# Right-hand tiles shifted by 32 bytes, and the last MLP chunk's down product without Strassen's scheme

## The chip, the cores and the metric

The kernel runs on one core of a Trainium2 chip. The time is the device time of one execution in microseconds; several executions were timed and the median is given. A profile of one execution goes with it.

## The reference, cut to what matters

One layer on 512 tokens of 1,024 features, in float32. The first half: RMSNorm, one input projection into five parts, a recurrent branch (causal convolution, gated linear recurrence, times a GeLU gate) and a spatial-gating branch, merged by two sigmoid gates and projected back. The second half is a squared-ReLU MLP of width 4,096, then a final RMSNorm:

```python
h2 = rmsnorm(x, norm_ffn_g)
f = jnp.square(jax.nn.relu(jnp.einsum('bsd,df->bsf', h2, w_up)))
x = x + jnp.einsum('bsf,fd->bsd', f, w_down)
out = rmsnorm(x, final_norm_g)
```

## The kernel before, in words

Every large product is done in three float32r matmuls: each operand is split into a high part (rounded to float32r) and a low part (the rest), and high x high, high x low and low x high are summed in PSUM (`mm3`, lines 239 to 242). Every matmul of these products is 128x128 by 128x512.

**Places in SBUF.** Tile pools are opened on the left side, growing up from low addresses, or on the right side (`side="right"`), growing down from the top. On the right lie only `xp` in the first half (24 tiles of 2,048 bytes per partition: `xg0` to `xg7` high and low, and `u`) and, after it is closed, `x2p` in its place (24 tiles: the residual `xres0` to `xres7` and `x20` to `x27` high and low). In the compiled program these begin at 180,192 and every 2,048 bytes from there; 180,192 leaves 32 when divided by 64. The pools on the left hold the weights (`wp`: `wraw`, `whi`, `wlo`), the first half's other tiles (`tp`, with `ya`, `yb`, `mg`) and the MLP's (`mp`); their tiles that a product reads leave 0, and these addresses are no part of the change.

**First half.** `v` and `u` (lines 307 to 321) have tokens on the partitions: `xg` is the stationary operand and the weights stream. The column tiles that follow in the order of `ORDER` (lines 32 to 35 and 554 to 566) have weights as the stationary operand: `x`, `g`, `gb` and `ga` stream `xg` (8 k-tiles, 24 matmuls per column tile), `bb` streams `yb` (24), `ba` streams `ya` (10 k-tiles, 30 matmuls), and `o` streams `mg` (24).

**Weights.** A list of items gives the order in which PE uses 512 KB weight tiles. `item()` (line 217) takes the next one, splits up to three items ahead and issues loads up to five ahead, on SP's queue. A split is one ACT pass for the high part (line 116) and one DVE subtraction for the low part (line 117). Items for which `by_dma` (line 189) holds, all `up` weights of the MLP and some of its last chunk's others, have ACT write the high part and its negative (lines 207, 208), and a DMA issued by POOL adds the raw tile to it (line 209).

**MLP.** The width is cut into four chunks of 1,024. In a chunk c, eight `up` steps (24 matmuls, streaming `x2`) make `f`; `up_out` (line 615) evacuates them with DVE and ACT. The down product of a chunk is done on 2x2 blocks (two token halves, two halves of the chunk's width, two halves of the output) in Strassen's scheme, Winograd's form: seven products (`PRODUCTS`: p1, p2, p5, p6, p3, p7, p4) of 24 matmuls each. Sums of activation blocks (`factor`, line 643) and of weight blocks (`sum_item`, line 176) are made by DVE in place ahead of them. Each product's activation block is split into `fh` and `fl`, which have two buffers each. After each product, DVE adds its two PSUM banks to the residual `xk` (line 701). The `up` steps of chunk c+1 stand between the products of chunk c (`mlp_steps`, line 60). The last chunk has no `up` steps between its products.

**End.** `last` (line 725) squares the residual with a row sum on ACT as parts of it are complete, and `finish` (line 713) makes, for each block of 128 tokens, the root of the mean square (DVE, ACT, DVE), then the two halves of the output on DVE, and writes each with a DMA.

The order of instructions on an engine is laid down at build time by a planner that simulates them; on the chip each engine's queue runs in that order.

Of the kernel before, what the change touches and what calls it, by code (L numbers as in the profile page):

```python
# [52 lines left out]
PRODUCTS = ("p1", "p2", "p5", "p6", "p3", "p7", "p4")  # L53
HK = KT // 2
HT = T // 2

AHEAD = 120


def mlp_steps():  # L60

    steps = [("up", 0, j) for j in range(FT)]
    for c in range(NCH):
        more = [("up", c + 1, j) for j in range(FT)] if c + 1 < NCH else []
        for q in PRODUCTS:
            steps.append(("dn", c, q))
            steps += more[:1]
            more = more[1:]
        steps += more
    return steps  # L70

# [2 lines left out]
def trunk(ctx: ExitStack, tc: tile.TileContext, xT, wall, wdn, lruw, wsT, par, ln, out):  # L74
    nc = tc.nc
# [59 lines left out]
    mp = [None]  # L135
# [11 lines left out]
    n_first = n_units - NCH * FT  # L147
    items = [("u", u) for u in range(n_first)]
    steps = mlp_steps()
    for s in steps:  # L150
        if s[0] == "up":
            items.append(("u", n_first + s[1] * FT + s[2]))
        else:
            items += [("d", s[1], s[2], h) for h in range(2)]
    raws, ready, summed = {}, {}, set()
    dn_raw = {}
# [31 lines left out]

    def by_dma(n):

        kind = items[n][0]
        return n >= n_first and (kind == "u" or (items[n][1] == NCH - 1 and items[n][2] in ("p2", "p6", "p3", "p4")))

    def split_item(n, pieces=1):
        if n >= len(items) or n in ready:
            return
        hi = wp.tile([P, UB * P], F32R, tag="whi", name=f"whi{n}", bufs=4)
        lo = wp.tile([P, UB * P], F32R, tag="wlo", name=f"wlo{n}", bufs=4)
        if items[n][0] == "u":
            src = raws.pop(n)  # L200
        else:
            _, c, q, h = items[n]
            sum_item(n)
            src = dn_raw[c, {"p1": "b11", "p2": "b21", "p5": "b12", "p6": "b12", "p3": "b22", "p7": "b11", "p4": "b21"}[q], h]
        if by_dma(n):

            nc.scalar.activation(hi, src, AF.Copy)  # L207
            nc.scalar.activation(lo, hi.bitcast(F32), AF.Copy, scale=-1.0)  # L208
            nc.gpsimd.dma_start(out=lo, in_=src, accum_op=ALU.add)  # L209
        else:  # L210
            w = UB * P // pieces
            for i in range(pieces):
                sl = slice(i * w, (i + 1) * w)
                split(src[:, sl], hi[:, sl], lo[:, sl])
        ready[n] = (hi, lo)

    def item():
        n = pos[0]
        pos[0] += 1
        ready.pop(n - 1, None)  # L220
        ahead = 3 if n < n_first - 1 else 4
        for i in range(ahead):
            split_item(n + i)
        for i in range(ahead, ahead + 2):
            sum_item(n + i)
        for i in range(ahead, 6):
            load_item(n + i)
        return ready[n]
# [128 lines left out]
    lw = []  # L357
# [282 lines left out]
        tick()  # L640


    def factor(c, q):
        a = a_[c]
        if q in ("p5", "p6"):
            a["s" + q[1]] = mp[0].tile([P, HK, HT], F32, tag="fs", name=f"s{c}{q}", bufs=2)
        for out_, in0, in1, op in {
            "p5": [("s5", "a21", "a22", ALU.add)],
            "p6": [("s6", "s5", "a11", ALU.subtract)],
            "p3": [("a12", "a12", "s6", ALU.subtract)],  # L650
            "p7": [("a11", "a11", "a21", ALU.subtract)],
        }.get(q, []):
            nc.vector.tensor_tensor(out=a[out_], in0=a[in0], in1=a[in1], op=op)
        src = a[{"p1": "a11", "p2": "a12", "p5": "s5", "p6": "s6", "p3": "a12", "p7": "a11", "p4": "a22"}[q]]
        hi, lo = (mp[0].tile([P, HK, HT], F32R, tag=f"f{x}", name=f"f{x}{c}{q}", bufs=2) for x in "hl")
        split(src, hi, lo)
        return hi, lo

    fac, bank = {}, {}

    def ahead_of(i):

        for s in steps[i + 1 :]:
            if s[0] == "dn":
                c, q = s[1:]
                if (c, q) not in fac and made[c] >= (HK if q == "p1" else FT):
                    fac[c, q] = factor(c, q)
                return

    def down(i, c, q, done):  # L670
        if (c, q) not in fac:
            fac[c, q] = factor(c, q)

        k = {"p1": "d", "p6": "d", "p7": "d", "p4": "d", "p2": "e", "p5": "e", "p3": "e"}[q]
        first = q in ("p1", "p2", "p5")
        if first:
            bank[k] = [(pd if k == "d" else pe).tile([P, T], F32, tag=k, name=f"{q}{c}_{j}") for j in range(2)]
        w = [item(), None]
        fh, fl = fac.pop((c, q))
# [12 lines left out]
        mm(1, 0)  # L692
        w[1] = item()
        mm(0, 1)
        mm(1, 1)
        ahead_of(i)
# [5 lines left out]
        done(q)  # L702


    gfin = [None]
    s3 = const.tile([P, NB, 2], F32, name="s3")
    r3 = const.tile([P, NB], F32, name="r3")

    def square(b, h):
        sq = mp[0].tile([P, T], F32, tag="fs", name=f"sqc{b}_{h}", bufs=2)  # L710
        nc.scalar.activation(sq, xk[b][h], AF.Square, accum_out=s3[:, b, h : h + 1])

    def finish(b):
        nc.vector.tensor_tensor(out=r3[:, b : b + 1], in0=s3[:, b, 0:1], in1=s3[:, b, 1:2], op=ALU.add)
        nc.scalar.activation(r3[:, b : b + 1], r3[:, b : b + 1], AF.Sqrt, bias=eps_t, scale=1.0 / D)
        nc.vector.reciprocal(r3[:, b : b + 1], r3[:, b : b + 1])
        for h in range(2):
            o = mp[0].tile([P, T], F32, tag="fa", name=f"o{b}_{h}", bufs=4)
            nc.vector.scalar_tensor_tensor(
                out=o, in0=xk[b][h], scalar=r3[:, b : b + 1], in1=gfin[0][:, h * T : (h + 1) * T],  # L720
                op0=ALU.mult, op1=ALU.mult,
            )
            (nc.sync, nc.scalar)[h].dma_start(out=out[b * P : (b + 1) * P, h * T : (h + 1) * T], in_=o)

    def last(q):

        for b, h in {"p2": [(0, 0), (1, 0)], "p3": [(0, 1), (1, 1)], "p7": [(2, 1), (3, 1)], "p4": [(2, 0), (3, 0)]}.get(q, []):
            square(b, h)
        for b in {"p3": (0, 1), "p4": (2, 3)}.get(q, ()):
            finish(b)  # L730

    t_stack.close()
    ps_stack.close()
# [7 lines left out]
    for i, step in enumerate(steps):  # L741
        if step[0] == "up":
            up(*step[1:])
            ahead_of(i)
        else:
            down(i, *step[1:], last if step[1] == NCH - 1 else lambda q: None)
    assert pos[0] == len(items) and block[0] == UB


# [73 lines left out]
```

## Time and profile before

| | us |
|---|---|
| median of 3 runs | 817.94 (817.55 to 818.36) |
| the profiled execution | 817.47 |
| its span | 815.5 |
| PE busy | 799.1 (98%) |
| DVE busy | 502.7 (62%) |
| ACT busy | 474.4 (58%) |

The span runs from the first to the last instruction of the profiled execution; the execution's own time is 1.97 us longer. Busy times count an engine's instructions; a matmul's recorded duration reaches into the next ones, so the step from one start to the next tells PE's rate, not the duration.

### The profile page before, as it was taken

Reading aid. Unit: us, or ns where it says so; the run is one execution under the profiler, and the core shown is the slowest. Engines: PE = TensorE matmul, PEld = TensorE weight load, DVE = VectorE, ACT = ScalarE, POOL = GpSimd, SP = SyncE. Lnnn points to the kernel's source line nnn. Section 1 sums busy time; section 2 is a strip of 40 time slices with the busy share of each in tenths; the row PEclk is TensorE's granted clock in tenths of the full one; section 3 lists DMA queues with packets and bytes.
Section 4 is the critical chain, followed back from the end, with each engine's and each line's share of the span. In section 5 each row is a group of like instructions: output and inputs, shape, how many; then the busy total and the mean of one; then the engine's idle time right before and its main releaser. Section 6 shows DMA issues by size and latency. Waiting matters only on the chain.

```text
span 815.5 us, 9147 instructions
## 1 busy us (share of the span) xinstructions
PE 799.1 (98%) x3472; PEld 648.4 (80%) x3472; DVE 502.7 (62%) x656; ACT 474.4 (58%) x573; POOL 72.5 (9%) x83
## 2 busy tenths in 40 slices
PE   9999999999999999999999999999999999999975
PEld 7788888888888888888888877888888888888854
DVE  6767764876566667745544232965487647754675
ACT  7455437768788887772334644645555545554563
POOL 5100000000000000000003300000000000000110
PEclk9999999999999999999999999999999999999989
DMA  7633331213322322232224894466545664564345
GB/s 254 200 104 110 96 117 52 103 66 104 114 80 84 110 103 104 79 116 86 96 101 148 208 307 155 102 170 182 165 103 152 184 181 101 131 204 107 62 93 155
DMA packets 31867, 105.77 MB, mean 130 GB/s; under 512 B 3792, under 2 KB 3792, under 8 KB 31824
## 3 DMA queue, kind: packets, MB, share of 16 engines
q1 hardware_dynamic: 22608, 77.66, 27.1%
q0 software_dynamic: 5760, 20.97, 13.5%
q10 hardware_dynamic: 3456, 6.56, 2.6%
q8 instruction: 27, 0.44, 0.2%
q14 instruction: 16, 0.13, 0.0%
HBM read 82.11 MB, written 2.10 MB: 103 GB/s over the span
## 4 chain that ended last, share of the span: by engine, by line
PE 91%; DMA 3%; DVE 2%; issue 2%; ACT 2%; SPq 0%; DVEq 0%; POOL 0%; POOLq 0%; ACTq 0%
PE p L686 16%; PE up L240 7%; PE up L241 7%; PE up L242 7%; PE v L315 6%; PE u L315 5%; PE g L241 2%; PE g L242 2%; PE x L240 2%; PE x L241 2%; PE x L242 2%; PE g L240 2%; PE ba L240 2%; PE ba L242 2%; PE ba L241 2%; PE ga L242 2%
## 5 line engine op out<-in xcount | busy, mean ns | idle before, releaser
L116 ACT ACTIVATE whi<-wraw 128x1024 fp32r<-128x1024 f32 (+1 forms) x79 | 82.2, 1044 | 83.4 <-issue 24.3
L117 DVE TENSOR_TENSOR wlo<-wraw,whi 128x1024 fp32r<-128x1024 f32 (+1 forms) x79 | 97.3, 1233 | 27.9 <-ACT whi L116 27.5
L624 DVE SCALAR_TENSOR_TENSOR f<-up,r_b 128x512 f32<-128x512 f32 x32 | 21.9, 688 | 66.1 <-PE up L242 65.8
L207 ACT ACTIVATE whi<-wraw 128x1024 fp32r<-128x1024 f32 x32 | 33.6, 1051 | 42.0 <-PE up L241 26.7
L209 POOL DMA_DIRECT2D wlo<-wraw x32 | 27.6, 862 | 259.4 <-ACT wlo L208 234.8
L515 DVE SCALAR_TENSOR_TENSOR w<-w,s 128x512 f32<-128x512 f32 x10 | 6.9, 692 | 59.7 <-ACT w L510 59.7
L208 ACT ACTIVATE wlo<-whi 128x1024 fp32r<-128x1024 f32 x40 | 42.0, 1053 | 0.7
L701 DVE TENSOR_TENSOR xk<-p,xk 128x512 f32<-128x512 f32 x56 | 36.9, 683 | 5.4 <-PE p L686 5.4
L116 ACT ACTIVATE whi<-raw1b 128x1024 fp32r<-128x1024 f32 x14 | 14.9, 1062 | 25.4 <-PE up L241 15.6
L116 ACT ACTIVATE whi<-raw2b 128x1024 fp32r<-128x1024 f32 x14 | 14.9, 1061 | 24.5 <-PE up L241 15.6
L116 ACT ACTIVATE whi<-raw0b 128x1024 fp32r<-128x1024 f32 x14 | 14.8, 1058 | 22.4 <-PE up L241 15.3
L511 POOL TENSOR_TENSOR ig<-ig,xr 128x512 f32<-128x512 f32 x10 | 12.9, 1291 | 161.8 <-ACT ig L505 148.0
L686 PE MATMUL p<-whi,fh3p 128*128 128x512 f32 x56 | 22.7, 417 | 4.7 <-ACT fh3p L116 4.7
L628 ACT ACTIVATE f<-f 128x512 f32<-128x512 f32 x32 | 20.0, 626 | 7.7 <-DVE f L624 7.7
L117 DVE TENSOR_TENSOR wlo<-raw1b,whi 128x1024 fp32r<-128x1024 f32 x14 | 17.1, 1224 | 10.0 <-ACT whi L116 9.8
L686 PE MATMUL p<-wlo,fh3p 128*128 128x512 f32 x56 | 22.8, 406 | 0.5 <-DMA wlo<-raw3b 0.5
L479 DVE SCALAR_TENSOR_TENSOR xr<-xrp,par_sb,xr 128x512 f32<-128x512 f32 x30 | 22.5, 749 | 0.7
L117 DVE TENSOR_TENSOR wlo<-raw2b,whi 128x1024 fp32r<-128x1024 f32 x14 | 17.1, 1223 | 9.3 <-ACT whi L116 9.0
L485 ACT ACTIVATE xra<-xr 64x512 fp32r<-64x512 f32 x10 | 6.3, 632 | 27.3 <-DVE xr L479 27.3
L686 PE MATMUL p<-whi,fl3p 128*128 128x512 f32 x56 | 22.1, 407 | 0.0
L686 PE MATMUL p<-whi,fh0p 128*128 128x512 f32 x56 | 21.9, 391 | 0.0
L686 PE MATMUL p<-wlo,fh2p 128*128 128x512 f32 x56 | 21.8, 390 | 0.0
(852 smaller groups left out, 2445.5 us busy)
## 6 DMA issues: line engine op xcount, KB each, us to landing
wraw<-in_wall SPq DMA_DIRECT2D x109, 512.0 KB, 3.3
wlo<-wraw POOLq DMA_DIRECT2D x32, 512.0 KB, 4.5
raw0b<-in_wdn SPq DMA_DIRECT2D x8, 512.0 KB, 14.4
raw1b<-in_wdn SPq DMA_DIRECT2D x8, 512.0 KB, 4.1
raw2b<-in_wdn SPq DMA_DIRECT2D x8, 512.0 KB, 4.2
raw3b<-in_wdn SPq DMA_DIRECT2D x8, 512.0 KB, 4.3
wlo<-raw3b POOLq DMA_DIRECT2D x8, 512.0 KB, 4.6
xt<-in_xT SPq DMA_DIRECT2D x8, 256.0 KB, 6.5
```

Of the source, the lines that this page charges most:

```text
L116: nc.scalar.activation(hi, src, AF.Copy)
L117: nc.vector.tensor_tensor(out=lo, in0=src, in1=hi.bitcast(F32), op=ALU.subtract)
L207: nc.scalar.activation(hi, src, AF.Copy)
L208: nc.scalar.activation(lo, hi.bitcast(F32), AF.Copy, scale=-1.0)
L209: nc.gpsimd.dma_start(out=lo, in_=src, accum_op=ALU.add)
L240: nc.tensor.matmul(acc, lhs[0], rhs[0], start=start, stop=False)
L241: nc.tensor.matmul(acc, lhs[0], rhs[1], start=False, stop=False)
L242: nc.tensor.matmul(acc, lhs[1], rhs[0], start=False, stop=stop)
L315: nc.tensor.matmul(acc[b], xg[k][xi][:, b * P : (b + 1) * P], w[wi], start=k == 0 and i == 0, stop=k == KT - 1 and i == 2,)
L479: nc.vector.scalar_tensor_tensor(out=xr, in0=xrp[:, 1 + k : 1 + k + T], scalar=pc(C_CW + k * RT + j), in1=xr, op0=ALU.mult, op1=ALU.add)
L686: nc.tensor.matmul(bank[k][j], lhs[li], rhs[ri], start=first and kk == 0 and n == 0, stop=kk == HK - 1 and n == 2, skip_group_check=True,)
L701: nc.vector.tensor_tensor(out=x, in0=bank[k][j], in1=x, op=ALU.add)
```

## The change

A pool of one tile of 32 bytes per partition is opened on the right side ahead of all others there, so that every right-hand tile starts 32 bytes lower, at a multiple of 64.

In the MLP's last chunk the seven products are replaced by eight block products (`whole`), each over all four blocks of 128 tokens: for each half of the output (nh) and of the chunk's width (kh), two weight tiles (half) of 24 matmuls. No sums of blocks are made there. The activation blocks are split once each, four splits (`factor_whole`): the high parts take the buffers of `fh` (kh = 0) and `fl` (kh = 1), the low parts two buffers of `fa`. The accumulators are four banks, from `pe` for the first output half, and from `pd` and `pu` for the second. In the last of the four weight tiles of an output half the blocks of tokens end one by one, and each is added to the residual, squared and, in the second half, finished as it ends. The last chunk's `up` steps all stand ahead of chunk 2's p4, two of them after p3.

`by_dma` now holds only for the `up` weights of chunks 1 to 3; the first chunk's and all the last chunk's down weights are split by ACT and DVE. The splits and sums of activations are called from `item()`, by the item that is two (splits) or five (sums) ahead, and no longer after each step. In `finish` the first output half is made by ACT from the residual that DVE has multiplied by the final gain earlier, the second by DVE as before.

```diff
+        if c + 1 == NCH:
+            steps += [("whole", c, kh, nh, half) for nh in range(2) for kh in range(2) for half in range(2)]
+            break
...
+            if c + 2 == NCH and q == "p4":
+                steps += more
+                more = []
             steps.append(("dn", c, q))
-            steps += more[:1]
-            more = more[1:]
+            n = 2 if c + 2 == NCH and q == "p3" else 1
+            steps += more[:n]
+            more = more[n:]
...
+    padp = ctx.enter_context(tc.tile_pool(name="padp", bufs=1, side="right"))
+    pad = padp.tile([P, 8], F32, name="pad")
+    nc.vector.memset(pad, 0.0)
...
     def by_dma(n):
-        kind = items[n][0]
-        return n >= n_first and (kind == "u" or (items[n][1] == NCH - 1 and items[n][2] in ("p2", "p6", "p3", "p4")))
+        return n >= n_first + FT and items[n][0] == "u"
...
         ahead = 3 if n < n_first - 1 else 4
-        for i in range(ahead):
-            split_item(n + i)
-        for i in range(ahead, ahead + 2):
-            sum_item(n + i)
+        for i in range(6):
+            ahead_of(n + i, i < 3)
+            if i < ahead:
+                split_item(n + i)
+            else:
+                sum_item(n + i)
...
+    def factor_whole(c, kh):
+        if (kh, 0) in whole_f or made[c] < (kh + 1) * HK:
+            return
+        los = mp[0].tile([P, 2, HK, HT], F32R, tag="fa", name=f"lw{kh}", bufs=4)
+        for th in range(2):
+            src = a_[c][f"a{th + 1}{kh + 1}"]
+            hi = mp[0].tile([P, HK, HT], F32R, tag="fhfl"[2 * kh : 2 * kh + 2], name=f"fw{kh}{th}", bufs=2)
+            lo = los[:, th]
+            split(src, hi, lo)
+            whole_f[kh, th] = (hi, lo)
+
+    def hidden(n, whole):
+        if whole and n < len(items) and items[n][0] == "w":
+            factor_whole(items[n][1], int(items[n][2][1]) - 1)
+        if n < len(items) and items[n][0] == "d" and items[n][3] == 0:
+            c, q = items[n][1:3]
+            if made[c] >= (HK if q == "p1" else FT):
+                (factor if whole else factor_sum)(c, q)
...
+    def whole(c, kh, nh, half):
+        w = item()
+        if kh == 0 and half == 0:
+            for b in range(NB):
+                pool, tag = ((pe, "e"), (pd, "d"), (pu, "up"))[nh * (1 + b // 2)]
+                bank[b] = pool.tile([P, T], F32, tag=tag, name=f"w{nh}_{b}")
+        end = kh == 1 and half == 1
+
+        def mm(b, k):
+            fh, fl = (x[:, 2 * half + k, b % 2 * P : (b % 2 + 1) * P] for x in whole_f[kh, b // 2])
+            wh, wl = (x[:, k * T : (k + 1) * T] for x in w)
+            for n, (l, r) in enumerate(((fh, wh), (fh, wl), (fl, wh))):
+                nc.tensor.matmul(
+                    bank[b], l, r, start=kh == 0 and half == 0 and k == 0 and n == 0, stop=end and k == 1 and n == 2
+                )
+
+        if not end:
+            for k in range(2):
+                for b in range(NB):
+                    mm(b, k)
+            return
+        for b in range(NB):
+            for k in range(2):
+                mm(b, k)
+            x = xk[b][nh]
+            with tc.high_priority(offset=AHEAD):
+                nc.vector.tensor_tensor(out=x, in0=bank[b], in1=x, op=ALU.add)
+                square(b, nh)
+                if nh == 1:
+                    finish(b)
...
         for h in range(2):
-            o = mp[0].tile([P, T], F32, tag="fa", name=f"o{b}_{h}", bufs=4)
-            nc.vector.scalar_tensor_tensor(
-                out=o, in0=xk[b][h], scalar=r3[:, b : b + 1], in1=gfin[0][:, h * T : (h + 1) * T],
-                op0=ALU.mult, op1=ALU.mult,
-            )
+            o = og[b // 2][:, b % 2, h]
+            if h == 0:
+                nc.scalar.activation(o, xk[b][h], AF.Copy, scale=r3[:, b : b + 1])
+            else:
+                nc.vector.scalar_tensor_tensor(
+                    out=o, in0=xk[b][h], scalar=r3[:, b : b + 1], in1=gfin[0][:, T:], op0=ALU.mult, op1=ALU.mult
+                )
             (nc.sync, nc.scalar)[h].dma_start(out=out[b * P : (b + 1) * P, h * T : (h + 1) * T], in_=o)
```

## Rows read from the trace of the kernel before

**Rows 1.** The page, busy us (share of the span) xinstructions, and the chain that ended last.

```profile
PE 799.1 (98%) x3472; PEld 648.4 (80%) x3472; DVE 502.7 (62%) x656; ACT 474.4 (58%) x573; POOL 72.5 (9%) x83
...
PE 91%; DMA 3%; DVE 2%; issue 2%; ACT 2%; SPq 0%; DVEq 0%; POOL 0%; POOLq 0%; ACTq 0%
```

**Rows 2.** Waits of PE, whole span: who waited for whom, us, times, longest.

```profile
PE p L686 <- ACT fh3p L116: 4.7, 2, 3.5
PE up L240 <- DVE f L624: 1.9, 1, 1.9
...
PE p L686 <- DMA wlo<-raw3b: 0.5, 1, 0.5
```

**Rows 3.** Timeline of PE in u, gb and up: start us, us, instruction.

```profile
52.72 0.62 PE L315 MATMUL u<-whi,xg0h 128*128 128x512 f32 x2
...
97.52 0.39 PE L240 MATMUL gb<-xg0h,whi 128*128 128x512 f32 x1
...
187.65 0.39 PE L240 MATMUL gb<-xg0h,whi 128*128 128x512 f32 x1
...
193.27 0.39 PE L240 MATMUL g<-xg0h,whi 128*128 128x512 f32 x1
...
505.69 0.39 PE L240 MATMUL up<-x21h,whi 128*128 128x512 f32 x1
...
510.38 0.39 PE L242 MATMUL up<-x27h,wlo 128*128 128x512 f32 x1
```

**Rows 4.** Instructions on tiles o and ba: duration ns min/median/max, first and last start.

```profile
L240 PE MATMUL o<-mg0h,whi x8: 389/389/390, 416.0 to 454.1; 128*128 128x512 f32 x8
...
L240 PE MATMUL ba<-ya0h,whi x8: 389/390/392, 361.6 to 409.2; 128*128 128x512 f32 x8
```

**Rows 5.** Groups by line, PE's transposes: busy us, mean ns, idle before.

```profile
L443 PE MATMUL ybT<-ident,ybt 128*128 128x128 f32 x32 | 4.8, 272 | 0.0
...
L608 PE MATMUL x2T<-ident,xres 128*128 128x128 f32 x32 | 4.5, 272 | 0.0
```

**Rows 6.** Timeline of PE in the last chunk's products.

```profile
760.41 0.39 PE L686 MATMUL p<-whi,fh3p 128*128 128x512 f32 x1
...
780.46 0.50 PE L686 MATMUL p<-whi,fh3p 128*128 128x512 f32 x1 [3.52 <-ACT fh3p L116]
...
783.30 1.22 PE L686 MATMUL p<-whi,fh3p 128*128 128x512 f32 x2 [1.19 <-ACT fh3p L116]
...
787.31 0.63 PE L686 MATMUL p<-whi,fl3p 128*128 128x512 f32 x1
787.73 0.44 PE L686 MATMUL p<-whi,fh3p 128*128 128x512 f32 x1
...
804.88 0.50 PE L686 MATMUL p<-wlo,fh3p 128*128 128x512 f32 x1 [0.54 <-DMA wlo<-raw3b]
```

**Rows 7.** Groups by line and shape, a weight tile's split on ACT and DVE.

```profile
L117 DVE TENSOR_TENSOR wlo<-wraw,whi 128x1024 fp32r<-128x1024 f32 x77 | 95.9, 1247 | 27.1 <-ACT whi L116 26.8
L116 ACT ACTIVATE whi<-wraw 128x1024 fp32r<-128x1024 f32 x77 | 81.0, 1055 | 82.4 <-issue 24.3 <-PE ba L241 18.2 <-PE u L315 9.0
```

**Rows 8.** Windows: us, PE, PEld, DVE, ACT, POOL busy (x), PEclk, DMA share, GB/s.

```profile
230.00:300.00 70.00, 70.00 (x304) 56.73 (x303) 46.67 (x60) 58.39 (x69) 4.17 (x6) 1.00 0.28 98
459.50:482.00 22.50, 22.50 (x108) 18.19 (x107) 6.09 (x5) 15.24 (x20) 3.80 (x4) 1.00 0.95 261
760.40:807.45 47.05, 41.80 (x169) 32.71 (x167) 35.29 (x42) 29.09 (x40) 6.02 (x7) 0.93 0.50 105
```

**Rows 9.** Timeline of DVE at the end.

```profile
807.48 0.69 DVE L701 TENSOR_TENSOR xk<-p,xk 128x512 f32<-128x512 f32 x1 [0.44 <-PE p L686]
...
809.41 1.42 DVE L719 SCALAR_TENSOR_TENSOR o<-xk,r,gfin 128x512 f32<-128x512 f32 x2
...
810.93 1.41 DVE L719 SCALAR_TENSOR_TENSOR o<-xk,r,gfin 128x512 f32<-128x512 f32 x2
```

**Rows 10.** Timeline of DVE in the first chunk's up steps.

```profile
485.94 1.23 DVE L187 TENSOR_TENSOR raw0b<-raw0b,raw0b 128x1024 f32<-128x1024 f32 x1 [11.18 <-DMA raw0b<-in_wdn]
```

More of the change, by code (lines that the diff above doesn't have):

```diff
@@ L64, in mlp_steps @@
         more = [("up", c + 1, j) for j in range(FT)] if c + 1 < NCH else []
-        for q in PRODUCTS:
+        if c + 1 == NCH:
+            steps += [("whole", c, kh, nh, half) for nh in range(2) for kh in range(2) for half in range(2)]
+            break
+        order = PRODUCTS
+        for q in order:
+            if c + 2 == NCH and q == "p4":
+                steps += more
+                more = []
             steps.append(("dn", c, q))
-            steps += more[:1]
-            more = more[1:]
+            n = 2 if c + 2 == NCH and q == "p3" else 1
+            steps += more[:n]
+            more = more[n:]
         steps += more
@@ L152, in trunk @@
             items.append(("u", n_first + s[1] * FT + s[2]))
+        elif s[0] == "whole":
+            items.append(("w", s[1], f"b{s[2] + 1}{s[3] + 1}", s[4]))
         else:
@@ L203, in split_item @@
             sum_item(n)
-            src = dn_raw[c, {"p1": "b11", "p2": "b21", "p5": "b12", "p6": "b12", "p3": "b22", "p7": "b11", "p4": "b21"}[q], h]
+            src = dn_raw[c, {"b11": "b11", "b21": "b21", "b12": "b12", "b22": "b22", "p1": "b11", "p2": "b21", "p5": "b12", "p6": "b12", "p3": "b22", "p7": "b11", "p4": "b21"}[q], h]
         if by_dma(n):
@@ L215, in split_item, with ahead_of @@
         ready[n] = (hi, lo)
+    prep = [None]
+    def ahead_of(n, whole):
+        if prep[0] is not None:
+            prep[0](n, whole)
     def item():
@@ L640, in up, with factor_sum @@
         tick()
-    def factor(c, q):
+    fsum, fac, bank = set(), {}, {}
+    def factor_sum(c, q):
+        if (c, q) in fsum:
+            return
+        fsum.add((c, q))
         a = a_[c]
@@ L653, in factor, with down @@
             nc.vector.tensor_tensor(out=a[out_], in0=a[in0], in1=a[in1], op=op)
-        src = a[{"p1": "a11", "p2": "a12", "p5": "s5", "p6": "s6", "p3": "a12", "p7": "a11", "p4": "a22"}[q]]
+    def factor(c, q):
+        if (c, q) in fac:
+            return
+        factor_sum(c, q)
+        src = a_[c][{"p1": "a11", "p2": "a12", "p5": "s5", "p6": "s6", "p3": "a12", "p7": "a11", "p4": "a22"}[q]]
         hi, lo = (mp[0].tile([P, HK, HT], F32R, tag=f"f{x}", name=f"f{x}{c}{q}", bufs=2) for x in "hl")
         split(src, hi, lo)
[L657 to L672, printed above, removed]
+        fac[c, q] = (hi, lo)
+    whole_f = {}
+    def factor_whole(c, kh):
+        if (kh, 0) in whole_f or made[c] < (kh + 1) * HK:
+            return
+        los = mp[0].tile([P, 2, HK, HT], F32R, tag="fa", name=f"lw{kh}", bufs=4)
[12 more added lines that the diff above has]
+                (factor if whole else factor_sum)(c, q)
+    def down(c, q):
         k = {"p1": "d", "p6": "d", "p7": "d", "p4": "d", "p2": "e", "p5": "e", "p3": "e"}[q]
@@ L678, in down @@
         w = [item(), None]
-        fh, fl = fac.pop((c, q))
+        fh, fl = fac[c, q]
         def mm(j, h):
@@ L695, in down @@
         mm(1, 1)
-        ahead_of(i)
         th, nh = {"p1": (0, 0), "p2": (0, 0), "p5": (1, 1), "p6": (0, 1), "p3": (0, 1), "p7": (1, 1), "p4": (1, 0)}[q]
@@ L701, in down @@
                 nc.vector.tensor_tensor(out=x, in0=bank[k][j], in1=x, op=ALU.add)
-        done(q)
-    gfin = [None]
+    def whole(c, kh, nh, half):
[16 more added lines that the diff above has]
+                    mm(b, k)
+            return
+        for b in range(NB):
[7 more added lines that the diff above has]
+                    finish(b)
+    gfin, og = [None], [None, None]
     s3 = const.tile([P, NB, 2], F32, name="s3")
@@ L709, in square @@
     def square(b, h):
-        sq = mp[0].tile([P, T], F32, tag="fs", name=f"sqc{b}_{h}", bufs=2)
-        nc.scalar.activation(sq, xk[b][h], AF.Square, accum_out=s3[:, b, h : h + 1])
+        if h == 0 and b % 2 == 0:
+            og[b // 2] = mp[0].tile([P, 2, 2, T], F32, tag="fa", name=f"o{b // 2}", bufs=4)
+        nc.scalar.activation(og[b // 2][:, b % 2, h], xk[b][h], AF.Square, accum_out=s3[:, b, h : h + 1])
+        if h == 0:
+            nc.vector.tensor_tensor(out=xk[b][h], in0=xk[b][h], in1=gfin[0][:, 0:T], op=ALU.mult)
     def finish(b):
@@ L717, in finish @@
         for h in range(2):
-            o = mp[0].tile([P, T], F32, tag="fa", name=f"o{b}_{h}", bufs=4)
-            nc.vector.scalar_tensor_tensor(
-                out=o, in0=xk[b][h], scalar=r3[:, b : b + 1], in1=gfin[0][:, h * T : (h + 1) * T],
-                op0=ALU.mult, op1=ALU.mult,
-            )
-            (nc.sync, nc.scalar)[h].dma_start(out=out[b * P : (b + 1) * P, h * T : (h + 1) * T], in_=o)
[L725 to L730, printed above, removed]
+            o = og[b // 2][:, b % 2, h]
+            if h == 0:
+                nc.scalar.activation(o, xk[b][h], AF.Copy, scale=r3[:, b : b + 1])
[3 more added lines that the diff above has]
+                )
+            (nc.sync, nc.scalar)[h].dma_start(out=out[b * P : (b + 1) * P, h * T : (h + 1) * T], in_=o)
     t_stack.close()
@@ L740, in trunk @@
     a_ = [{} for _ in range(NCH)]
-    for i, step in enumerate(steps):
+    prep[0] = hidden
+    for step in steps:
         if step[0] == "up":
             up(*step[1:])
-            ahead_of(i)
+        elif step[0] == "whole":
+            whole(*step[1:])
         else:
-            down(i, *step[1:], last if step[1] == NCH - 1 else lambda q: None)
+            down(*step[1:])
     assert pos[0] == len(items) and block[0] == UB
```

## The prediction

> **What bounds the kernel now.** I read the page's busy shares and chain first, then the waits of PE, then single rows of PE's timeline stage by stage. PE is busy 98% of the span and carries 91% of the chain [rows 1]; the waits that the trace lays at its door are few: 4.7 us for ACT and 0.5 us for a DMA in the last chunk's products, 1.9 us for DVE at one place in the first chunk [rows 2]. So the time is the number of matmuls times the step from one start to the next, plus what the last chunk and the end lose. DVE and ACT stand behind it: in a stage heavy for both, 230 to 300 us, ACT is busy 58.4 of 70 us [rows 8].
>
> The reader is to look at the step, not at the durations. The granted clock is 1.00 in both windows shown outside the last chunk [rows 8], yet there are two steps. A `gb` column tile (24 matmuls) lies between 187.65 and 193.27: 5.62/24 = 234.2 ns. In `up`, 20 steps from 505.69 to 510.38 make 234.5 ns. `u` takes 52.72 to 97.52 for 192 matmuls: 233.3 ns [rows 3]. But `o` from its first to its eighth column (7 x 24 = 168 steps, 416.0 to 454.1) makes 226.8 ns, and `ba` (7 x 30 = 210 steps, 361.6 to 409.2) 226.7 ns [rows 4]. What separates them is where an operand lies. `gb` and `up` stream `xg` and `x2` tiles from the right-hand pool; `u` has `xg` as its stationary operand; `o` and `ba` take both operands from left-hand pools. In the program of before every right-hand tile starts at a remainder of 32 modulo 64, every left-hand operand of these products at 0. So a right-hand operand in either role goes with some 7 ns per matmul.
>
> **The change part by part**, against the profiled execution's 817.47 us (span 815.5 and 1.97 around it; the median of the runs is 817.94, 0.47 above).
>
> *The pad.* 32 bytes at the top of the right side move both right-hand pools to a remainder of 0; the left ones stay. Products with a right-hand operand: `x` 10, `g` 10, `gb` 8, `ga` 8 and `up` 32 column tiles of 24, 1,632 matmuls with it as the moving operand; `v` and `u`, 384 with it as the stationary one. Expected step: that of the left-hand tiles, about 226.8. 1,632 x (234.2 - 226.8) = 12.1 us and 384 x (233.3 - 226.8) = 2.5 us, 14.6 in all. Bounds: 0 if the address is not the cause, 14.6 if it is; no loss, since left-hand tiles at the remainder 0 already make the shorter step. I take 14.5. The cover: ACT's 58.4 us of work per 70 us [rows 8] would then lie in 67.8, so PE stays the later one. The memset is one small DVE operation ahead of all work. Against it stand the transposes: those that read `xres` (right) and those that read `ybt` (left) both show 272 ns [rows 5]; but they have 128 columns, so they need not be bound by the same thing.
>
> [...]
>
> *Last chunk, `whole`.* [...] After, 8 block products are 192 x 226.8 = 43.5 us. Preparation falls: 8 weight splits and 4 factor splits instead of 14 and 7, no weight sums, no factor sums, no accumulating DMA. With an ACT part of 1.06 and a DVE part of 1.25 us each [rows 7], the twelve cost 12.7 and 15.0 us, under 43.5 of PE work. One wait is new: the second token half of the first factor takes the `fh` buffer of `p4`, so its ACT split can begin only when `p4` has ended. PE covers this with six matmuls of blocks 0 and 1 (6 x 0.227 = 1.36), block 2's third matmul comes 0.45 later, and the split takes about 0.2 to be released + 1.06 + 1.25 = 2.5: a wait of 0.7 us. Queued behind that split on ACT are later weight splits, already needed only 5.4 us per item. Steps moved in chunk 2 (two `up` after `p3`, the last one ahead of `p4`) issue the same splits and loads; the SP queue has no weight load left behind them that PE soon needs. Term: 43.5 + 0.7 - 47.05 = -2.8 us. Bounds: -3.5 (no wait) to +1 (waits as long as 3.52 and 1.19 stay). I take -2.8.
>
> *The end.* Before, from the last matmul's evacuation at 807.48 to the end of the last output product at 812.34 (810.93 + 1.41) are 4.86 us: one addition (0.69), four output products on DVE (1.42 and 1.41 for two each), 1.3 for square and small steps [rows 9]. After, only block 3 is left: one addition, one output product on DVE, the other on ACT. Gone is 0.7 (block 3's second product) to 2.1 (block 2's too). DVE's work per block (0.69 + 0.71 + some 0.5) is above PE's 1.36, so it may lag by up to 0.7 us: bounds -2.1 to +0.7. I take -1.0.
>
> *First chunk's `up` weights* lose the accumulating DMA: their low part goes from an ACT pass plus a DMA to DVE (1.25 us). Before, a DVE subtraction on `raw0b` stood 11.18 us for its load, with the DMA rings 0.95 busy (459.5 to 482), and held the evacuation for which PE waited 1.9 us [rows 2, 8, 10]. Fewer bytes then should bring that load earlier; but now weight splits can stand behind the same subtraction. Bounds -1.9 to +2; I take -1.0.
>
> Sum: 817.47 - 14.5 - 2.8 - 1.0 - 1.0 = 798.2; with the 0.47 by which the median is above, 798.6. I say 798.5 us.
>
> **The rivals.**
> - *The shift gains nothing*, because the right side is slow for where it lies and not for its remainder, or because the pad does not move the pools: only the other terms remain, 817.94 - 4.8 = 813.1. For it: the transposes [rows 5]. Against it: one step for all right-hand products, in two roles, and another for all left-hand ones [rows 3, 4]. Chance 0.09. [...]
> - *Only the moving operand gains*: `v` and `u` stay at 233.3; 2.5 us less gain, 801.0. For it: their stationary loads are hidden behind the matmuls. Against it: their step is as far above 226.8 as the others'. Chance 0.10.
> - *Slower: the last chunk starves.* ACT's queue is in order, and the split that waits for `p4` blocks the weight splits behind it; PE stands, its clock falls. One such episode, waits and slow steps together, cost 8.9 - 0.5 = 8.4 us in the kernel before [rows 6, 8]. From three of them in `whole`'s eight steps the 19.4 us are gone: 798.5 + 3 x 8.4 = 823.7. Against it: four weight buffers ahead, 12 splits in 43.5 us. Chance 0.02.
> - *The gain is taken by ACT or DVE behind a faster PE*, at most the difference of 2.1 us per 70 in the stages with 58 us of ACT: some 8 us over 100 to 360, 806. Chance 0.04, as ACT has 9 us left there.
>
> **How the numbers follow.** The forecast has 0.75, with its own range of 795.5 to 801.5 (the bounds of the three small terms seldom meet). The 801.0 case and half of the 806 case belong to the range of 795 to 804; outside it lie the 813 case, the slower case and the edges, under 0.2. A measurement of this kernel tells about 0.2% (1.6 us) from no change. Faster by more: 0.96; within: 0.01; slower: 0.03 (the starving case, and 0.01 that I have not thought of).
>
> **What would show it.** The pad: `gb`, `up` and `u` at a step of 227 ns, `o` and `ba` unchanged; a step still at 234 refutes the largest term. `whole`: 192 matmuls within 44.5 us at a clock of 1.00, with one wait of about 0.7 us before block 2. The end: from the last evacuation to the last output product under 4 us. First chunk: no wait of PE for DVE near 475 us. The prediction is wrong if PE shows long waits at places where before it had none.

## The result and the profile after

| | before | after |
|---|---|---|
| median, us | 818.04 (817.55 to 818.36, 4 runs) | 810.29 (809.49 to 810.61, 4 runs) |
| ratio | | 0.9904 (0.9887 to 0.9921) |
| the profiled execution, us | 817.47 | 810.42 |
| its span, us | 815.5 | 808.6 |

The change gains 7.75 us where 19.4 were forecast. The time lies above the range of 795 to 804.

The page after, first its busy shares, then the chain that ended last (they answer to [rows 1]):

```profile
PE 798.5 (99%) x3496; PEld 650.9 (80%) x3496; DVE 493.6 (61%) x646; ACT 452.4 (56%) x552; POOL 61.1 (8%) x67
...
PE 98%; DMA 0%; DVE 0%; ACT 0%; SPq 0%; issue 0%; ACTq 0%
```

PE is now the chain almost alone: 98% where it was 91%. Yet its busy time fell by only 0.6 us, with 24 more matmuls in it (0.7%, 5.4 us at 227 ns). The waits are gone; the matmuls of the right-hand products are still slow. All the waits of PE that are left (engine, line, whom it waited for: us, times, longest):

```profile
PE warm L120 <- DVE sp L421: 1.1, 1, 1.1
PE v L337 <- ACT whi L129: 0.6, 1, 0.6
```

Neither is at one of the places of [rows 2]. Now the steps. PE's timeline after, in `u`, a `gb` tile and `up`, each from a start to a start (start us, us, instruction), against [rows 3]:

```profile
52.80 0.39 PE L337 MATMUL u<-whi,xg0h 128*128 128x512 f32 x1
...
97.42 0.40 PE L262 MATMUL gb<-xg0h,whi 128*128 128x512 f32 x1
...
187.22 0.40 PE L262 MATMUL gb<-xg0h,whi 128*128 128x512 f32 x1
...
192.81 0.40 PE L262 MATMUL g<-xg0h,whi 128*128 128x512 f32 x1
...
502.33 0.39 PE L262 MATMUL up<-x21h,whi 128*128 128x512 f32 x1
...
507.00 0.39 PE L264 MATMUL up<-x27h,wlo 128*128 128x512 f32 x1
```

`gb`: (192.81 - 187.22) / 24 = 232.9 ns, before 234.2. `up`: 4.67 / 20 = 233.5, before 234.5. `u`: 44.62 / 192 = 232.4, before 233.3. The products with two left-hand operands stay at 227 (the tile view: duration ns min/median/max, first and last start; against [rows 4]): `o` 38.0 us / 168 = 226.2, `ba` 47.7 / 210 = 227.1 (starts to 0.1 us, so to about 0.5 ns).

```profile
L262 PE MATMUL o<-mg0h,whi x8: 389/389/389, 415.1 to 453.1; 128*128 128x512 f32 x8
...
L262 PE MATMUL ba<-ya0h,whi x8: 389/389/392, 360.6 to 408.3; 128*128 128x512 f32 x8
```

The last chunk and the first chunk's `up` stage as windows after (us, then PE, PEld, DVE, ACT, POOL busy (x), PEclk, DMA share, GB/s; against [rows 8]):

```profile
457.00:480.00 23.00, 23.00 (x111) 18.68 (x110) 11.58 (x11) 11.43 (x17) 2.09 (x2) 1.00 0.78 285
756.64:800.00 43.36, 43.36 (x192) 35.69 (x191) 16.70 (x24) 11.64 (x21) 0.00 (x0) 1.00 0.00 1
```

In the second PE is busy throughout, at a clock of 1.00 (before 0.93). The eight block products, first start to last end on PE's timeline, against [rows 6]:

```profile
756.48 0.39 PE L757 MATMUL w<-whi,fw 128*128 128x512 f32 x1
...
799.77 0.39 PE L757 MATMUL w<-whi,lw 128*128 128x512 f32 x1
```

192 matmuls in 43.68 us (756.48 to 800.16), a step of 43.29 / 191 = 226.7 ns; before, 168 took 47.04 (760.41 to 807.45). DVE at two places after, the first chunk's subtraction and the end (timeline; against [rows 9, 10]), and the writes of the output from issue to landing (their tile view):

```profile
477.24 1.23 DVE L202 TENSOR_TENSOR raw0b<-raw0b,raw0b 128x1024 f32<-128x1024 f32 x1 [2.67 <-DMA raw0b<-in_wdn]
...
800.37 0.68 DVE L771 TENSOR_TENSOR xk<-w,xk 128x512 f32<-128x512 f32 x1
...
803.64 0.75 DVE L797 SCALAR_TENSOR_TENSOR o<-xk,r,gfin 128x512 f32<-128x512 f32 x1
```

```profile
L800 ACTq DMA_DIRECT2D out_y<-o x4: 339/346/353, 800.5 to 804.4; - x4
L800 SPq DMA_DIRECT2D out_y<-o x4: 333/338/348, 801.1 to 804.4; - x4
...
DMA to landing us min/median/max: 2.0/2.3/3.1
```

The subtraction waits 2.67 us for its load instead of 11.18, and PE waits for no evacuation there. At the end, 800.37 to 804.39 are 4.02 us (4.86 before), but from there to the end of the span pass 4.2 us (3.16 before, 812.34 to 815.5).

### The profile page after: what moved, and what is told of

It reads as the page before. It is cut to its first block, busy times and chain, and to the rows that moved or that the text cites. A ratio compares the mean times of both kernels' runs of the same rounds, so it can differ in the third digit from the quotient of the medians.

```text
span 808.6 us, 9094 instructions
## 1 busy us (share of the span) xinstructions
PE 798.5 (99%) x3496; PEld 650.9 (80%) x3496; DVE 493.6 (61%) x646; ACT 452.4 (56%) x552; POOL 61.1 (8%) x67
## 4 chain that ended last, share of the span: by engine, by line
PE 98%; DMA 0%; DVE 0%; ACT 0%; SPq 0%; issue 0%; ACTq 0%
PE p L728 14%; PE up L264 7%; PE up L262 7%; PE up L263 7%; PE v L337 6%; PE u L337 6%; PE w L757 5%; PE g L262 2%; PE g L264 2%; PE x L264 2%; PE x L262 2%; PE g L263 2%; PE x L263 2%; PE ba L263 2%; PE ba L264 2%; PE ba L262 2%
## 5 line engine op out<-in xcount | busy, mean ns | idle before, releaser
L129 ACT ACTIVATE whi<-wraw 128x1024 fp32r<-128x1024 f32 (+1 forms) x87 | 90.5, 1045 | 108.5 <-issue 43.6
L130 DVE TENSOR_TENSOR wlo<-wraw,whi 128x1024 fp32r<-128x1024 f32 (+1 forms) x87 | 107.0, 1232 | 35.6 <-ACT whi L129 35.5
L221 ACT ACTIVATE whi<-wraw 128x1024 fp32r<-128x1024 f32 x24 | 25.2, 1051 | 26.7 <-PE up L263 26.7
L742 DVE TENSOR_TENSOR xk<-p,xk 128x512 f32<-128x512 f32 x42 | 27.3, 681 | 0.0
L222 ACT ACTIVATE wlo<-whi 128x1024 fp32r<-128x1024 f32 x24 | 25.4, 1057 | 0.5
L757 PE MATMUL w<-whi,fw 128*128 128x512 f32 x64 | 24.9, 389 | 0.0
L757 PE MATMUL w<-wlo,fw 128*128 128x512 f32 x64 | 24.9, 389 | 0.0
L757 PE MATMUL w<-whi,lw 128*128 128x512 f32 x64 | 24.7, 389 | 0.0
L728 PE MATMUL p<-wlo,fh0p 128*128 128x512 f32 x56 | 21.8, 390 | 0.0
L728 PE MATMUL p<-wlo,fh1p 128*128 128x512 f32 x56 | 21.8, 390 | 0.0
```

Of the source, the lines that this page charges most:

```text
L130: nc.vector.tensor_tensor(out=lo, in0=src, in1=hi.bitcast(F32), op=ALU.subtract)
L728: nc.tensor.matmul(bank[k][j], lhs[li], rhs[ri], start=first and kk == 0 and n == 0, stop=kk == HK - 1 and n == 2, skip_group_check=True,)
L757: nc.tensor.matmul(bank[b], l, r, start=kh == 0 and half == 0 and k == 0 and n == 0, stop=end and k == 1 and n == 2)
```

## The experiments

Most of them are on the largest term, the pad; the last three are on the others. Steps of bare matmuls are means over 36 steps, from the 9th to the 45th start of a group of 48, at a granted clock of 1.00 in every stretch read; a group's first steps are uneven, and from its first to its last start the mean differs by up to 1.9 ns. Ratios are to the kernel before, run beside each on its chip; its median was 817.4 to 818.2 us on the three chips.

**Which property of the address counts.** The kernel keeps only matmuls of the products' shape (three per k-tile as in `mm3`) over one large tile, with chosen addresses for both operands; the layer itself is left out. An entry is a group's name, the address of its moving operand and that of its stationary one.

```diff
+LOW = 36160
+for i, d in enumerate((0, 16, 32, 64, 96, 128, 160, 192, 256, 320, 384, 448)):
+    CONF.append((f"m{'abcdefghijkl'[i]}", 100672 + d, LOW))
+for i, (m, d) in enumerate(((182592, 0), (182592, 128), (200000, 0), (200000, 128), (209728, 0), (209728, 128))):
...
+    ("sa", 100352, LOW - 320),
+    ("sb", 100352 + 128, LOW - 320),
+    ("sc", 100672 + 64, LOW + 64),
+    ("sd", 100672, LOW + 128),
```

> The kernel leaves out all of the reference's work: it fills SBUF with data and runs 26 groups of 48 matmuls (128x128 by 128x512, float32r, a new stationary block each time, as in a column tile), each group with its own addresses; the step from start to start is read. Groups ma to ml: stationary at 320 modulo 512, moving operand near 100,000 at 320 + 0, 16, 32, 64, 96, 128, 160, 192, 256, 320, 384, 448. Groups ha to hf: moving operand near 182,000, 200,000 and 209,000, at +0 and +128 each. Groups sa, sb, sc: both operands shifted, sa and sc alike, sb apart by 128; sd, rb, rd: the stationary one shifted by 128. Theory REGION (operands from 180,000 up are read more slowly): 227 ns in all m and s groups, 233 in all h groups, whatever the shift. Theory PHASE (what counts is how far apart the two operands lie modulo a power of two up to 512): 227 in ma, ha, hc, he, sa, sc, ra, rc; 233 or so in mc to ml except where the shift is a multiple of that power, 233 in hb, hd, hf, sb, sd, rb, rd. Theory OWN REMAINDER (each operand's address modulo 256 or 512 by itself): as PHASE in the m and h groups, but sa and sc at 233 too. Theory CONTENT (it is the data or what other engines do meanwhile): 227 everywhere.

The tile view of six groups (duration ns, first and last start):

```profile
L112 PE MATMUL ha<-big x48: 388/389/397, 148.9 to 159.5; 128*128 128x512 f32 x48
L112 PE MATMUL hb<-big x48: 387/394/398, 159.8 to 170.7; 128*128 128x512 f32 x48
...
L112 PE MATMUL sa<-big x48: 387/389/398, 215.1 to 225.8; 128*128 128x512 f32 x48
L112 PE MATMUL sb<-big x48: 387/394/399, 226.1 to 237.0; 128*128 128x512 f32 x48
L112 PE MATMUL sc<-big x48: 387/389/398, 237.2 to 247.9; 128*128 128x512 f32 x48
L112 PE MATMUL sd<-big x48: 389/392/404, 248.2 to 259.1; 128*128 128x512 f32 x48
```

`ha` and `hb` both stream from above 182,000, where the right-hand tiles lie: 226.7 and 233.3 ns. So it is not the place. DVE, ACT and POOL are idle and the DMA share is 0.00 from 148.9 to 259.3, so it is nothing that they do meanwhile either. Group `sa` has both operands 320 bytes lower, at other remainders, and keeps 226.8; `sc` has both 64 higher and keeps 226.7; `sb` and `sd`, where one operand lies 128 bytes from the other's phase, make 233.3 and 232.3. So it is not either operand's own remainder, but the distance between the two. With the places of the operands exchanged (`ra` to `rd`, the stationary one at 200,000 or at 100,000) it is the same: 226.7 at equal phase, 232.4 with 128 bytes between them. The first eight groups ran while the data was still being written and are not read here; a later run repeats them.

**What this says of the kernel.** The left-hand operands leave 320 modulo 512, the right-hand ones left 480 (180,192) and leave 448 with 32 bytes of pad. Modulo 256 the distance of a right-hand tile from a left-hand one was 160 and became 128; a pad of 160 bytes makes it 0. Four kernels test that: after with 160 bytes, with none, with 96 (distance 64) and with 416 (distance 256).

```diff
-    pad = padp.tile([P, 8], F32, name="pad")
+    pad = padp.tile([P, 40], F32, name="pad")
```

> The changed kernel with a pad of 160 bytes instead of 32: right-hand tiles leave 320 modulo 512, as the left-hand ones do (448 with 32 bytes, 480 without). REGION and CONTENT: the step of up, gb and u stays at 233 and the time at 810.3. PHASE and OWN REMAINDER: 227, so 2,016 x 6.2 ns = 12 us less than the changed kernel, 798.

Measured: 798.30 us (798.20 to 799.35), ratio 0.9764 (0.9750 to 0.9777). PE's timeline with 160 bytes, first the start of `u` and of the first `gb` tile behind it, then one `gb` tile to the next and an `up` tile of the second chunk:

```profile
51.75 1.07 PE L337 MATMUL u<-whi,xg0h 128*128 128x512 f32 x4
...
95.27 0.39 PE L262 MATMUL gb<-xg0h,whi 128*128 128x512 f32 x1
...
183.59 0.39 PE L262 MATMUL gb<-xg0h,whi 128*128 128x512 f32 x1
...
189.03 0.39 PE L262 MATMUL g<-xg0h,whi 128*128 128x512 f32 x1
...
505.63 0.39 PE L262 MATMUL up<-x21h,whi 128*128 128x512 f32 x1
...
510.16 0.39 PE L264 MATMUL up<-x27h,wlo 128*128 128x512 f32 x1
```

`u`: 43.52 / 192 = 226.7 ns; `gb`: 5.44 / 24 = 226.7; `up`: 4.53 / 20 = 226.5. The page of the same kernel: PE's busy time falls from 798.5 to 786.8 us with the same 3,496 matmuls.

```profile
PE 786.8 (99%) x3496; PEld 650.5 (82%) x3496; DVE 492.3 (62%) x646; ACT 451.7 (57%) x552; POOL 60.2 (8%) x67
```

Without the pad (its three lines left out):

> The changed kernel without the pad: right-hand tiles again at 32 modulo 64. If the pad is worth the difference of the steps read from the two traces (234.2 to 233.1 in column tiles, 233.6 to 232.4 in u and v: 2,016 x 1.1 ns), the time is 810.3 + 2.2 = 812.5; if the pad is worth nothing, 810.3.

Measured: 812.00 us (811.84 to 812.46), ratio 0.9930 (0.9917 to 0.9944). And the kernel before with those three lines alone:

> The kernel before with the 32-byte pad alone. If the pad is worth 2.2 us: 815.8; if nothing: 818.0; if, as I forecast, the pad alone carried the gain: 803.5.

Measured: 816.60 us (815.64 to 818.20), ratio 0.9985 (0.9975 to 0.9994). By both, the change's pad is worth 1.4 to 1.7 us, and the rest of the change about 6.0 (818.0 - 812.0).

`[P, 24]`, a distance of 64:

> The changed kernel with a pad of 96 bytes: right-hand tiles lie 64 bytes past the left-hand ones modulo 256 (128 past with 32 bytes, 0 with 160). By the step of 228.9 ns that the bare matmuls showed at a distance of 64, PHASE gives 798.3 + 2,016 x 2.2 ns = 802.7. A theory by which only the distance 0 helps and all others cost alike (233): 810.3.

Measured: 805.74 us (805.56 to 805.99), ratio 0.9850 (0.9835 to 0.9864), 3 us above what was expected. `up` makes 229.4 ns in the mean (226.7 to 231.9 by line); but `v` and `u`, which have the shifted operand as the stationary one, stay at 233.7 and 233.3. Seen from them the distance is -64, that is 192, and the sweep below has 233.3 there. Their 384 matmuls by 4.4 ns are 1.7 us of the 3. The rest is in products that have no right-hand operand but follow one that has: `p` makes 228.75 ns (226.7 with 160 bytes) and `bb` 228.7 (227.1), over 696 matmuls 1.3 us. Only the first steps of such a tile are slow, here a `p` tile behind an `up` tile, its 1st, 11th and 24th matmul:

```profile
526.62 0.40 PE L728 MATMUL p<-whi,fh0p 128*128 128x512 f32 x1
...
528.94 0.39 PE L728 MATMUL p<-wlo,fh0p 128*128 128x512 f32 x1
...
531.88 0.39 PE L728 MATMUL p<-whi,fl0p 128*128 128x512 f32 x1
```

The first ten steps are 232 ns in the mean, the other thirteen 226. So a distance is still felt for some matmuls after it has changed.

`[P, 104]`, a distance of 256:

> The changed kernel with a pad of 416 bytes: right-hand tiles leave 64 modulo 512, so that they differ from the left-hand ones by 256. PHASE with a period of 256: 226.8 ns and 798.3, as with 160 bytes. PHASE with a period of 512: a longer step, 803 or more.

Measured: 798.65 us (797.91 to 799.48), ratio 0.9763 (0.9748 to 0.9778), with 226.7 to 227.3 ns in the mean of every right-hand product. The period is 256 bytes or a divisor of it; 128 and 64 are ruled out by the kernel after and by the 96-byte pad.

**The curve.** Bare matmuls again, the layer left out; the stationary operand stays and the moving one shifts.

```diff
+for i in range(16):
+    CONF.append((f"m{'abcdefghijklmnop'[i]}", 100672 + 16 * i, LOW))
+for i, d in enumerate((4, 8, 256, 512, 1024, 1024 + 128, 2048 + 64)):
+    CONF.append((f"n{'abcdefg'[i]}", 100672 + d, LOW))
```

> The kernel leaves out all of the reference's work, as the first one of bare matmuls, and runs its groups one after the other once all data is in place. Stationary operand at 320 modulo 512, moving operand at 320 + 0, 16, ..., 240 (ma to mp), and + 4, 8, 256, 512, 1024, 1152, 2112 (na to ng); the first group z is at the distance 0 elsewhere. PHASE with a period of 256: 226.8 at 0, 256, 512, 1024; 228.9 at 64 and at 2112 (64 modulo 256); 233 at 128 and at 1152; between 228 and 235 elsewhere. A theory of lines of 64 bytes: 64, 128 and 192 like 0, all others longer.

| distance, bytes | 0 | 4 | 8 | 16 | 32 | 48 | 64 | 80 | 96 | 112 | 128 |
|---|---|---|---|---|---|---|---|---|---|---|---|
| step, ns | 226.9 | 238.1 | 233.3 | 231.7 | 233.3 | 233.3 | 228.9 | 231.1 | 233.3 | 231.1 | 232.6 |

| distance, bytes | 144 | 160 | 176 | 192 | 208 | 224 | 240 | 256 | 512 | 1024 | 1152 | 2112 |
|---|---|---|---|---|---|---|---|---|---|---|---|---|
| step, ns | 233.3 | 234.3 | 233.3 | 233.3 | 234.8 | 233.3 | 226.7 | 226.7 | 226.7 | 226.7 | 233.3 | 228.9 |

Five of these groups in the tile view (distances 0, 64, 128, 160 and 256, in this order):

```profile
L100 PE MATMUL ma<-big x48: 387/389/398, 39.7 to 50.4; 128*128 128x512 f32 x48
...
L100 PE MATMUL me<-big x48: 388/392/397, 84.1 to 94.9; 128*128 128x512 f32 x48
...
L100 PE MATMUL mi<-big x48: 390/393/404, 128.5 to 139.4; 128*128 128x512 f32 x48
...
L100 PE MATMUL mk<-big x48: 388/397/400, 150.9 to 161.9; 128*128 128x512 f32 x48
...
L100 PE MATMUL nc<-big x48: 389/389/398, 240.5 to 251.1; 128*128 128x512 f32 x48
```

The bare steps give back those of the kernels, with the distance counted from the stationary to the moving operand: before, `gb` at 160 (234.2 in the kernel, 234.3 bare) and `u` at 96 (233.3 and 233.3); after, `gb` at 128 (232.9 and 232.6). Most distances cost 4 to 8 ns; 0 and 240 cost nothing, 64 costs 2.

**Which matmuls feel it.** Bare matmuls once more, the layer left out, at distances 0, 128 and 160 each: a new stationary block each time; the same one each time; 256 columns; 128 columns; the stationary operand shifted.

> Bare matmuls again; the kernel leaves out all of the reference's work. Moving operand at the distances 0, 128 and 160 (x, y, z): group a with a new stationary block each time and 512 columns, b with one stationary block for all, c and d with 256 and 128 columns, e with the stationary operand shifted and not the moving one. If the distance costs something per weight load that runs beside a moving stream: a 226.8, 233, 234; c and d longer by the same 6 to 7 ns at 128 and 160 than at 0; b the same as a if the stationary block is loaded again all the same, or no difference between its three if it is not. If it costs something per column streamed: c longer by 3.3, d by 1.6. Group e: 226.8, then about 232.4.

| | 0 | 128 | 160 |
|---|---|---|---|
| 512 columns, ns | 226.7 | 233.3 | 234.3 |
| 512, the same stationary block | 226.7 | 233.3 | 234.3 |
| 256 columns | 120.0 | 118.7 | 117.3 |
| 128 columns | 111.7 | 111.7 | 111.7 |
| 512, stationary shifted | 226.9 | 232.4 | 233.3 |

Distances 0 and 128 for 256 and 128 columns (tile view):

```profile
L107 PE MATMUL cx<-big x48: 281/283/283, 107.7 to 113.3; 128*128 128x256 f32 x48
L107 PE MATMUL cy<-big x48: 279/281/285, 113.4 to 119.0; 128*128 128x256 f32 x48
...
L107 PE MATMUL dx<-big x48: 219/275/280, 124.7 to 129.9; 128*128 128x128 f32 x48
L107 PE MATMUL dy<-big x48: 273/275/276, 130.1 to 135.3; 128*128 128x128 f32 x48
```

At 256 columns the sign turns, at 128 nothing is left. The transposes have 128 columns, and they fit this: their equal durations [rows 5] would not have told, but by their starts too both kinds step by 109 ns in the trace of before.

**The other terms.** First chunk: after with 160 bytes, and the first chunk's `up` weights made by the accumulating DMA again.

```diff
     def by_dma(n):
-        return n >= n_first + FT and items[n][0] == "u"
+        return n >= n_first and items[n][0] == "u"
```

> The kernel with the pad of 160 bytes, but the first chunk's up weights again split through the accumulating DMA. If the wait of 1.9 us for DVE in the first chunk came from that DMA's traffic, it is back and the time is 800.2; if it went for another reason (the order on DVE), 798.3.

Measured: 802.34 us (801.45 to 803.95), ratio 0.9810 (0.9795 to 0.9825), 4.0 us above the 160-byte version by the medians, 2.9 by the two profiled spans (799.3 and 796.4). That is 2.1 us above what was expected. The waits of PE hold the old one again, twice, and DVE's first subtraction on `raw0b` (its timeline) stands for its load again:

```profile
PE up L262 <- DVE f L646: 2.0, 2, 1.0
...
476.58 1.23 DVE L202 TENSOR_TENSOR raw0b<-raw0b,raw0b 128x1024 f32<-128x1024 f32 x1 [9.98 <-DMA raw0b<-in_wdn]
```

With 160 bytes alone the same subtraction stands 3.02 us. The wait comes back with the accumulating DMA and explains 2.0 us of the loss. By PE's timeline all of the 2.9 us between the profiled executions lies in this stage: PE is 0.1 us behind when the stage begins (458.3) and 2.9 when its first `p` begins (502.27 against 499.40). What makes up the other 0.9 us there stays open.

The kernel before with 160 bytes of pad alone:

> The kernel before with the pad of 160 bytes alone. PHASE: 1,632 x 7.4 + 384 x 6.7 ns = 14.6 us less, 803.4. A rival, by which ACT and DVE take part of it back once PE is faster: 805 to 810.

Measured: 805.67 us (805.50 to 806.66), ratio 0.9852 (0.9836 to 0.9869): 12.5 us gained against 14.6 by the steps. Its steps are 226.7 to 227.4 in the mean of every right-hand product; its waits are those of [rows 2], with the first chunk's grown from 1.9 to 2.5 us:

```profile
PE p L690 <- ACT fh3p L120: 4.3, 2, 3.6
PE up L244 <- DVE f L628: 2.5, 1, 2.5
...
PE p L690 <- DMA wlo<-raw3b: 0.6, 1, 0.6
```

Behind the longer wait the granted clock is lower for a few microseconds, 0.54 in the mean of the window below; in the kernel before it was 1.00 behind the shorter one (488 to 492). The window, with the columns of [rows 8]:

```profile
481.30:485.00 3.70, 3.70 (x10) 2.88 (x10) 1.54 (x2) 0.00 (x0) 0.00 (x0) 0.54 1.01 383
```

Nine steps from 481.36 to 485.01 take 3.6 us where nine of 227 ns take 2.0. The 0.6 us of wait and these 1.6 us make 2.2, where 2.1 are missing. So a faster PE reaches the same wait sooner and gives a part back. In the kernel after, where these waits are gone, the step from no pad to 160 bytes is worth 13.7 us (812.0 - 798.3).

The end: after with 160 bytes, and the last two weight tiles of the second output half used block by block, 12 matmuls of each block of tokens in a row instead of 6, so that the blocks end 2.7 us apart.

```diff
-        w = item()
+        held[half] = item()
...
-        end = kh == 1 and half == 1
+        late = kh == 1 and nh == 1
...
+        if late and half == 0:
+            return
...
-            for k in range(2):
-                mm(b, k)
+            for hf in range(2) if late else (1,):
+                for k in range(2):
+                    mm(b, hf, k)
```

> The kernel with the pad of 160 bytes, and the last two weight tiles of the second output half used block of tokens by block (12 matmuls each), so that the blocks end 2.7 us apart and not 1.36. If the end is late because four blocks' finishing work and eight output writes meet within 5 us (first evacuation of the last block to the last output product 4.0 us, the last write landing after 3.1): product 3.0, landing 2.1, so 796.3. If the end is only the last block's own chain: 798.3. If holding two weight tiles at once starves PE: above 798.3.

Measured: 796.84 us (796.66 to 797.04), ratio 0.9748 (0.9735 to 0.9761), the fastest version here. DVE's last addition and the two products behind it, and the landing of the writes:

```profile
788.43 0.69 DVE L777 TENSOR_TENSOR xk<-w,xk 128x512 f32<-128x512 f32 x1 [0.25 <-PE w L759]
789.04 0.74 DVE L803 SCALAR_TENSOR_TENSOR o<-xk,r,gfin 128x512 f32<-128x512 f32 x1
...
790.73 0.75 DVE L803 SCALAR_TENSOR_TENSOR o<-xk,r,gfin 128x512 f32<-128x512 f32 x1
```

```profile
L806 SPq DMA_DIRECT2D out_y<-o x4: 332/338/347, 783.2 to 791.5; - x4
L806 ACTq DMA_DIRECT2D out_y<-o x4: 339/346/360, 783.3 to 791.5; - x4
...
DMA to landing us min/median/max: 2.1/2.3/2.7
```

788.43 to 791.48 are 3.05 us where the 160-byte version takes 4.02, like the kernel after: behind the last addition DVE has one product of another block left to do (789.04), where the 160-byte version has two (789.06 and 790.06, behind an addition at 788.20). The writes are issued over 8 us instead of 4, and the slowest lands in 2.7 us instead of 3.1. Less the 0.23 us by which the last addition starts later, the two make 1.1 us, the gain in the span; but the intervals of the two ratios overlap, and the writes alone were not tried.

## Why the prediction was wrong

**The pad, -14.5 forecast, -1.4 to -1.7 measured: this step failed.** It read: "Expected step: that of the left-hand tiles, about 226.8." The count of matmuls and the gap of 7 ns were right, and the version with 160 bytes collects 13.7 of the 14.6 us. What failed is the inference from the rows. They separate products with a right-hand operand from those without [rows 3, 4]; I took for the cause the remainder modulo 64, one of several properties that set right-hand addresses apart. The remainder of an operand by itself does nothing (groups `sa` and `sc`, 226.8 and 226.7 ns); what counts is its distance from the other operand, and a shift from 160 to 128 (96 to 128 for `v` and `u`) leads from one slow distance to another (234.3 and 233.3 to 232.6 ns in the sweep). The rows at hand could not tell these apart: in the program of before right-hand tiles leave 480 modulo 512 and left-hand ones 320, without exception. The bounds read "0 if the address is not the cause, 14.6 if it is"; another slow address was not among the cases.

The rival *the shift gains nothing* gave 813.1, and the time is 2.8 below it. Its result was near, its reason was not: the right side is not slow for where it lies (`ha`, 226.7 ns from above 182,000). The rival *only the moving operand gains* is refuted by the 160-byte version, where `v` and `u` gain as well (`u` makes 226.7 ns, 232.4 after).

**Last chunk, -2.8 forecast, -3.4 measured** (43.68 against 47.04). Right, at the bound without a wait: the 0.7 us before block 2 did not come, and the clock stayed at 1.00. The prediction covered the split with six matmuls of blocks 0 and 1; in the program as built the planner puts 23 of them ahead of block 2's first, 5.2 us against the 2.5 reckoned for the split. The 0.2 us for the release in those 2.5 was an estimate; in the trace of before DVE begins on an `up` tile 0.43 us after the start of its last matmul (510.38 to 510.81), 0.20 more than a step. The rival in which the chunk starves did not occur; ACT is busy 11.6 of 43.4 us there. Its 8.9 us are the 47.05 of before less 168 steps of 226.8 ns (38.1): the waits of 3.52, 1.19 and 0.54 and the slow steps behind the first two [rows 6], 427 ns from 784.32 to 787.31, where the granted clock was 0.50 (784 to 787).

**First chunk, -1.0 forecast, about -1.9 measured.** The wait of PE is gone. The down weights' load lands earlier with less of the accumulating DMA, as reckoned: the subtraction stands 2.67 us for it instead of 11.18, and 9.98 with that DMA back (3.02 without, at the same pad). The other side of it, weight splits behind the same subtraction, cost PE nothing. Undone, it costs more than it took (2.9 to 4.0 us).

**The end, -1.0 forecast, +0.4 measured** (last matmul's end to the span's end: 807.45 to 815.5 are 8.05 us, 800.16 to 808.6 are 8.44). From the last evacuation to the last product 0.84 us are gained, nearly as reckoned, of which 0.18 are lost because DVE takes that evacuation 0.21 us after PE instead of 0.03. The term left out the writes: eight are now issued within 4 us, 800.5 to 804.4, and the last product's write lands 3.1 us after its issue, where before the writes were spread over 13 us (799.5 to 812.4) and the last took about 2.0. That the crowding makes them slow was not tried by itself, and it cannot be all: in the trace of before the slowest write took 3.2 us, and it was the third, issued 2.3 us after the second and 0.7 us before the fourth.

**ACT or DVE behind a faster PE** had no part: in the 160-byte version PE's page shows 99%, with no wait of PE for either that was not there after.

The sum of the four is -1.6 - 3.4 - 1.9 + 0.4 = -6.5, where the profiled executions differ by 7.05. By the steps themselves, in the mean over all these products in the two traces, the pad's term is larger, 1,632 x 1.1 (234.15 to 233.05) + 384 x 1.2 (233.6 to 232.4) ns = 2.3 us, and the sum -7.2. So the terms close to within what executions of one kernel differ by (809.49 to 810.61).

## What to carry to other kernels

When two classes of matmul differ in their step, list the addresses of both operands of each class before naming a cause, and try more than one shift: the first one tried here moved from one slow place to another, and 128 bytes more were worth 12 us (810.29 to 798.30). Where PE is the bound and a pool's start sets the distance between a product's operands, a pad is a cheap knob to sweep, for products of 512 columns. And at the end of a kernel, count the landing of the last writes as a term of its own when work is moved closer to it.

## What the runs showed of the hardware

- The step of back-to-back matmuls of 128x128 by 128x512 on float32r data depends on the distance between the addresses of the moving and the stationary operand, modulo 256 bytes (226.7 ns at 256, 512 and 1024 as well, 233.3 at 1152, 228.9 at 2112): 226.7 to 226.9 ns at 0 and 240, 228.9 at 64, 231 to 235 elsewhere at multiples of 16, 238.1 at 4. With 256 columns it is 120.0 at 0 and 117.3 at 160; with 128 columns 111.7 at each of three distances. It is the same with one stationary block as with new ones, when the block is loaded each time (48 loads of 188 ns).
- A distance is felt for some matmuls after it has changed: behind `up` at 64 the first ten steps of a `p` tile at 0 were 232 ns in the mean, the other thirteen 226 (96-byte pad).
- Why that is so stays open, and so does the turn of the sign at 256 columns (120.0 ns at 0, 117.3 at 160).
- A matmul's recorded duration hardly tells the two steps apart (389 ns at a step of 226.7, medians of 392 to 402 at the slow ones); the starts do.
